# Where matmul operands start in SBUF: moving the tiles of a hybrid decoder block onto multiples of 64 bytes

## The chip, the cores and the metric

The kernel runs on one core of one Trainium2 chip. The metric is the device time of one execution in microseconds, taken as the median of several runs. Two such kernels are compared here: the one called before, and the one that the change makes of it.

## The reference

One decoder block over 1024 tokens and 16 learned meta tokens (1040 in all), model width 1024, in float32. Cut to what matters:

```python
xn = rms_norm(h, norm_mix_g)
q, k, v, f_logit, b_gate, c_gate, u = split(xn @ w_in)       # 1024 -> 3*512 + 8 + 3*512
y_attn = forgetting_attention(q, k, v, log_sigmoid(f_logit + b_f))   # 8 heads of 64, causal
y_conv = b_gate * causal_depthwise_conv(c_gate * u, conv_w)          # 3 taps
h = h + concat(head_rms_norm(y_attn), head_rms_norm(y_conv)) @ w_out
a = square(relu(rms_norm(h, norm_mlp_g) @ w_ff1))                    # 1024 -> 4096
h = h + a @ w_ff2
return rms_norm(h, final_norm_g)[:, 16:]
```

## The kernel before, in words

A product is made of three matmuls. Each float32 operand is split into a high part (rounded to fp32r) and a low part (the rest), by `split` (lines 117 to 119): ScalarE casts the high part, VectorE or GpSimd subtracts. A product then is high times high, high times low and low times high, three matmuls of 128 rows into one PSUM bank, up to 512 columns each. The call is `matmul(out, stationary, moving)`: the stationary operand is a tile of 128 columns that is loaded into TensorE, the moving one is streamed past it. In the rows of the trace the two stand as `out<-moving,stationary`.

The work runs through these stages, which follow each other on TensorE:

- Up to 73 us: the tokens are normed and transposed into `xh` and `xl` (lines 222 to 230), and the values are projected (`value_tile`, line 255).
- 73 to 407 us: the projection of q, k and the three convolution inputs (`project`, line 469), first alone, then as filler between the small matmuls of attention (`scores` lines 531 to 534, `transposed` line 554, `weighted` lines 568 to 570). Here the weights are stationary (`wh`, `wl`) and the tokens move. The tokens of one group are cut into runs of columns by `chunks` (lines 333 to 336): 2 runs of 512 for q and for the convolution's gate, 3 of 348, 348 and 344 for k, 3 of 342 for the convolution's two other inputs, which begin 2 tokens early, at token 14. A run of 3 times 8 matmuls fills one of two PSUM banks named `mm`; after it the run is evacuated by ScalarE and VectorE into a page `pg`.
- 407 to 514 us: the rest of attention, with the convolution's half of the output projection as filler (`out_conv`, line 658).
- 514 to 604 us: the attention half of the output projection (`mixed`, line 863), the norm and the transposes for the MLP (line 877), and the first products of the MLP (`ahead`, line 993).
- 604 to 901 us: the first MLP matrix in Strassen form (`product`, line 993): 1272 matmuls of 512 columns one after the other. The token tiles `xa` to `xd` move, the weights (`wf0`, `ws12`, `ws43`, `wa22`) are stationary.
- 901 to 1205 us: the second MLP matrix in the same form (`second`, line 1298): 1344 matmuls of 512 columns. The weights `w2` move, the activations `a2` are stationary.

What sets the order: within attention the filler is a Python generator; `fill(us)` (lines 692 to 694) draws matmuls from it, and each tells its width over 2400 as its price (line 471), until the slot's quota (tables `QUOTA0` and `QUOTA1`) is used up. From there on TensorE's instructions are kept in the order in which the program names them; on the other engines a scheduler decides where it isn't pinned. The loads of the next group's weights (`wr`, line 329) and the stores of q and k (lines 399 to 415) stand in one queue, SP's.

Where a tile lies: pools take SBUF from the left end upwards, or (with `side="right"`) from the right end downwards, and each tile begins at the next multiple of 32 bytes in its partition. So a tile of an odd number of 32-byte pieces moves all that follow it by 32 bytes. In the program as built, the operands of the 5937 matmuls begin at these remainders by 64 bytes (for a slice of a tile, the slice's own start):

| matmuls | count | moving, stationary |
|---|---|---|
| line 1298: most steps; the second (`ws12`,`wf0`) and the last two | 1272; 72 | 32, 32; 0, 0 |
| line 993, `acc`; `ahead` | 1272; 72 | 32, 0; 32, 32 |
| line 863, `wa`,`y3`; `wa`,`yh` or `yl` | 48; 144 | 32, 0; 0, 0 |
| line 658 | 192 | 0, 0 |
| line 469, 512 columns | 384 | 0, 32 |
| line 469, 342 columns | 576 | 16, 40 or 56; 32 |
| line 469, 348 columns; 344 columns | 192; 96 | 0 or 48, 32; 32, 32 |
| line 255 | 416 | half 0, 0 and half 32, 0 |
| lines 531 and 532 | 224 | 0, 0 (104); 16, 32 or 48, 0 (120) |
| line 554 (transposes) | 320 | 110 at 0, 0; 210 at 0, 32 |

Of the kernel before, what the change touches and what calls it, by code (L numbers as in the profile page):

```python
# [11 lines left out]
F32 = mybir.dt.float32  # L12
F32R = mybir.dt.float32r
# [7 lines left out]
P = 128  # L21
# [15 lines left out]
def r32(ap):  # L37
    return ap.bitcast(F32)
# [3 lines left out]
def hymba_block(  # L42
# [8 lines left out]
    L = T + NM  # L51
    NT = T // P
    KD = D // P
    NH = b_f.shape[1]
# [9 lines left out]
    NK = NT + 1  # L64
    LAST = L - NT * P
    SCALE = HD ** -0.5
    KPAD = 4
# [6 lines left out]
        name=nc.get_next_instruction_name(), act_func_set_id=LN_EXP_SET, ins=[], outs=[]))  # L74

    const = ctx.enter_context(tc.tile_pool(name="const", bufs=1))
    small = ctx.enter_context(tc.tile_pool(name="small", bufs=4))
    scr = ctx.enter_context(tc.tile_pool(name="scr", bufs=1, space=DRAM))

    ident = const.tile([P, P], F32, name="ident")  # L80
    make_identity(nc, ident)
    identb = const.tile([P, P], BF16, name="identb")
# [8 lines left out]
    nc.vector.memset(r32(bones), 0.0)  # L91
    for j in range(2):
        nc.vector.memset(r32(bones[j * HD:(j + 1) * HD, j * HD:(j + 1) * HD]), 1.0)
    epsc = const.tile([P, 1], F32, name="epsc")
    nc.vector.memset(epsc, EPS)
    halfc = const.tile([P, 1], F32, name="halfc")
    nc.vector.memset(halfc, -0.5)
    onec = const.tile([P, 1], F32, name="onec")
    nc.vector.memset(onec, 1.0)
    og = const.tile([P, KD], F32, name="og")  # L100
    cw = const.tile([P, 3, NC], F32, name="cw")
# [4 lines left out]
    def pe(ins):  # L106
        return tc.keep_in_program_order(ins) if ORDERED[0] else ins
# [48 lines left out]
    rp = proj.enter_context(tc.tile_pool(name="rp", bufs=1, reuse_waits="tile"))  # L156
# [10 lines left out]
    early = ExitStack()  # L167
    ep = early.enter_context(tc.tile_pool(name="ep", bufs=1, side="right", reuse_waits="tile"))
    NV = DA + NH
    wvh = ep.tile([P, KD, NV], F32R, name="wvh")  # L170
    wvl = ep.tile([P, KD, NV], F32R, name="wvl")

    tokens = [(xf[t * P:(t + 1) * P], P, NM + t * P) for t in range(NT)] + [(meta_tokens, NM, 0)]
    xts = []
# [113 lines left out]
                load_tokens()  # L288


    lf = rp.tile([P, NK, NH], F32, name="lf")
    nc.vector.scalar_tensor_tensor(out=lf, in0=zt, scalar=-1.0, in1=zt, op0=ALU.mult, op1=ALU.max)
    nc.scalar.activation(lf, lf, AF.Exp, scale=-1.0)
    nc.scalar.activation(lf, lf, AF.Ln, bias=onec)
# [3 lines left out]
    at = ap.enter_context(tc.tile_pool(name="at", bufs=1, side="right", reuse_waits="tile"))  # L298
# [32 lines left out]
        return wh, wl  # L331

    def chunks(lo, n, parts):
        step = -(-n // parts)
        step += step % 2
        return [(lo + i, min(step, n - i)) for i in range(0, n, step)]

    pages = ExitStack()
    pt = pages.enter_context(tc.tile_pool(name="pt", bufs=1, reuse_waits="tile"))
# [11 lines left out]
    def head_norm(src, kt, c, e2=None):  # L351

        st = {}
        s = src[:, c * 512:(c + 1) * 512]

        def squares():
            sq = st["sq"] = at.tile([P, 512], F32, name="n_sq", bufs=1)
            nc.scalar.activation(sq, s, AF.Square)
            st["sh"] = at.tile([P, 512], F32R, name="n_sh", bufs=1)
            st["sl"] = at.tile([P, 512], F32R, name="n_sl", bufs=1)  # L360
            split(st["sh"], st["sl"], sq, nc.gpsimd)

        def scaled():
            ps = bank("mm")
            pe(nc.tensor.matmul(ps, bones, st["sh"], start=True, stop=False))
            pe(nc.tensor.matmul(ps, bones, st["sl"], start=False, stop=e2 is None))
            for t in range(4 if e2 is not None else 0):
                w = e2[:, t].rearrange("p a b -> p (a b)")
                pe(nc.tensor.matmul(ps[:, t * P:(t + 1) * P], w, ident, start=False, stop=t == 3))
            r = st["sq"]  # L370
            nc.scalar.activation(r, ps, AF.Ln, bias=epsc if e2 is None else 0.0, scale=1.0 / HD)
            nc.scalar.activation(r, r, AF.Exp, scale=-0.5)
            y = at.tile([P, 512], F32, name="n_y", bufs=1)
            nc.vector.scalar_tensor_tensor(
                out=y, in0=s, scalar=og[:, kt:kt + 1], in1=r, op0=ALU.mult, op1=ALU.mult)
            if kt < NP - 1:
                nc.sync.dma_start(y_att[c][kt], y)
            elif kt < NP:
                split(y3["h"][:, c * 512:(c + 1) * 512], y3["l"][:, c * 512:(c + 1) * 512], y)
            else:  # L380
                nc.sync.dma_start(y_conv[c][kt - NP], y)

        return [squares, scaled]


    def q_group(p):
        st = {}

        def evac(ps, t0, n):
            if not st:  # L390
                st["h"], st["l"] = page(st), page(st)
            o = slice(t0 - NM, t0 - NM + n)
            hi = st["h"][:, o].bitcast(F32R)
            nc.scalar.mul(hi, ps, SCALE)
            nc.vector.scalar_tensor_tensor(
                out=st["l"][:, o].bitcast(F32R), in0=ps, scalar=SCALE, in1=r32(hi), op0=ALU.mult, op1=ALU.subtract)

        def done():
            nc.sync.dma_start(q_scr[p, 0], st["h"][:, :T])
            nc.sync.dma_start(q_scr[p, 1], st["l"][:, :T])  # L400

        return p * P, chunks(NM, T, 2), evac, done
# [16 lines left out]
    def conv_groups(ct):  # L419
        st = {}  # L420
        p0 = NM - 2
        ch = chunks(p0, T + 2, 3)

        def evac_c(ps, t0, n):
# [71 lines left out]
    def stacks(h):  # L496
        p, j = divmod(h, 2)
        js = slice(j * HD, (j + 1) * HD)
        ka = at.tile([P, L + KPAD], F32R, name="ka", bufs=2)
        kb = at.tile([P, L + KPAD], F32R, name="kb", bufs=2)  # L500
        qa = at.tile([P, T], F32R, name="qa", bufs=2)
        qb = at.tile([P, T], F32R, name="qb", bufs=2)
        for dst, src in ((qa[:HD], q_scr[p, 0, js]), (ka[:HD, :L], k_scr[p, 0, js]),
                         (qa[HD:], q_scr[p, 1, js]), (ka[HD:, :L], k_scr[p, 0, js]),
                         (qb[:HD], q_scr[p, 0, js]), (kb[:HD, :L], k_scr[p, 1, js]),
                         (qb[HD:HD + 4], qrow[h]), (kb[HD:HD + 4, :L], krow[h])):
            nc.sync.dma_start(r32(dst), src)
        nc.gpsimd.memset(r32(ka[:, L:]), 0.0)
        nc.gpsimd.memset(r32(kb[:HD + 4, L:]), 0.0)
        return qa, qb, ka, kb  # L510
# [6 lines left out]
    def scores(i, st, s):  # L517

        qa, qb, ka, kb = st
        n = NM + P * (i + 1)  # L520
        nb = 2 * (i // 2) + 2
        qs = slice(i * P, (i + 1) * P)
        nch = -(-n // 512)
        pad = -n % (2 * nch)
        v = (n + pad) // nch
        w = max(v, 256)
        ps = pp.tile([P, 3, 512], F32, name="S", bufs=BANKS["S"])
        for c in range(nch):
            ks = slice(c * v, c * v + w)
            last = c == nch - 1  # L530
            pe(nc.tensor.matmul(ps[:, c, :w], qa[:, qs], ka[:, ks], start=True, stop=False))  # L531
            pe(nc.tensor.matmul(ps[:, c, :w], qb[:HD + 4, qs], kb[:HD + 4, ks], start=False, stop=not last))  # L532
            if last:
                pe(nc.tensor.matmul(ps[:, c, v - P - pad:v], identb, maskb[:, :P + pad], start=False, stop=True))  # L534
        ps = ps[:, :nch, :v]
        nm = small.tile([P, 1], F32, name="nm")
        nc.vector.tensor_reduce(nm, ps, axis=AX.XY, op=ALU.max, negate=True)  # L537
        pr = at.tile([P, L + KPAD], F32, name="pr", bufs=3)
        if n < nb * P:
            nc.gpsimd.memset(pr[:, n:nb * P], 0.0)  # L540
        nc.scalar.activation(  # L541
            pr[:, :n + pad].rearrange("p (a b) -> p a b", b=v), ps, AF.Exp, bias=nm, accum_out=s)
        return pr
# [31 lines left out]

    def attention_norm(p, c):
        ts = slice(4 * c, 4 * c + 4)
        se = at.tile([P, 4, 2], F32, name="se", bufs=1)
        nc.vector.tensor_scalar(se, sums[p][:, ts], HD * EPS, None, op0=ALU.mult)
        e2 = at.tile([P, 4, 2, HD], F32, name="e2", bufs=1)  # L580
        both = [t.unsqueeze(3).broadcast_to([P, 4, 2, HD]) for t in (se, sums[p][:, ts])]
        nc.gpsimd.tensor_tensor(out=e2, in0=both[0], in1=both[1], op=ALU.mult)
        pending.extend(head_norm(o[p], p, c, e2))
# [116 lines left out]
    ORDERED[0] = True  # L700
    fill(START)
    pr = scores(0, st[0], sums[0][:, 0, 0:1])
    late = None
    for t, (h, i) in enumerate(slots):
# [8 lines left out]
        if t + 1 < len(slots):  # L713
# [5 lines left out]
            pr = scores(i1, st[h1], sums[p1][:, i1, j1:j1 + 1])  # L719
# [230 lines left out]
    for i in range(2, NT):  # L950
        n = i - 2
# [32 lines left out]
    def acc(n=1):  # L984
        return [p2.tile([P, 512], F32, name="acc", tag="acc", bufs=8) for _ in range(n)]
# [120 lines left out]
    n, m = NT - 2, NT - 1  # L1106
# [195 lines left out]
    b = acc(4)  # L1302
# [3 lines left out]
    right = [ctx.enter_context(tc.tile_pool(name=n, bufs=1, side="right", reuse_waits="tile")) for n in ("sr", "r11", "sp")]  # L1306
# [16 lines left out]
    lo, hi = slice(0, HD2), slice(HD2, D)  # L1323
# [56 lines left out]
    for i in range(2, len(steps)):  # L1380
# [14 lines left out]
        if i >= 4 and rowq:  # L1395
            a, tt = rowq.popleft()
# [23 lines left out]
        if q == 0:  # L1420
            b = acc(4)
# [37 lines left out]
```

## Time and profile before

| | |
|---|---|
| median of 3 runs | 1211.78 us (1211.17 to 1214.83) |
| the profiled execution | 1215.61 us, of which the program's span is 1213.5 us |
| mean granted TensorE clock | 0.988 of 2.4 GHz |
| TensorE busy | 1170.1 us, 96% of the span |
| VectorE, ScalarE, GpSimd busy | 729.2, 544.2, 225.8 us |
| matmuls of line 1298, line 469 | 513.6 us, 434.6 us as sums of overlapping durations |

A matmul's duration in these tables runs from its start to the end of its result, and the next one starts before that, so durations overlap. The pace of a run of matmuls is read from the timeline instead: the start of one and the start of another some places later, divided by the number of places.

### The profile page before, as it was taken

How to read it: one execution, taken by the hardware profiler on the slowest of the kernel's cores; microseconds unless marked ns; L12 is line 12 of the kernel's file. 1: busy time of each engine (PE TensorE's matmuls, PEld its weight loads, DVE VectorE, ACT ScalarE, POOL GpSimd, SP SyncE). 2: the span in 40 equal slices, each digit the busy share in tenths (PEclk: the TensorE clock that was granted, in tenths of full speed). 3: DMA queues.
4: the chain of work that ended last, by engine and by line, in shares of the span. 5: the costliest groups of instructions: out<-in, count | busy, mean ns of one | idle time of the engine just before them, and what ended most of it. 6: DMA issues, size and time to landing. Idle time of an engine off the chain costs nothing.

```text
span 1213.5 us, 15649 instructions
## 1 busy us (share of the span) xinstructions
PE 1170.1 (96%) x5969; PEld 987.1 (81%) x5969; DVE 729.2 (60%) x979; ACT 544.2 (45%) x910; POOL 225.8 (19%) x223
## 2 busy tenths in 40 slices
PE   6999999999999899978899999999999999999997
PEld 6988989899988777867788888888888888888886
DVE  7632354435354655549868766666664546985686
ACT  6522334553555554536544343435353433434444
POOL 3011132222221211212533332313100000000000
PEclk9999999999999899989999999999999999999999
DMA  8348242452324564255345444353559756432561
GB/s 259 132 145 234 71 91 57 120 153 61 90 88 141 156 190 130 72 182 182 120 130 191 145 142 165 122 184 102 191 197 363 276 205 228 154 104 70 173 243 70
DMA packets 119978, 185.91 MB, mean 153 GB/s; under 512 B 9536, under 2 KB 61760, under 8 KB 119904
## 3 DMA queue, kind: packets, MB, share of 16 engines
q1 hardware_dynamic: 119904, 184.92, 47.6%
q8 instruction: 47, 0.77, 0.3%
q14 instruction: 27, 0.22, 0.1%
HBM read 126.30 MB, written 58.59 MB: 152 GB/s over the span
## 4 chain that ended last, share of the span: by engine, by line
PE 87%; DVE 5%; DMA 4%; ACT 3%; issue 2%; POOL 0%; SPq 0%; DVEq 0%; ACTq 0%; POOLq 0%
PE acc L1298 25%; PE acc L993 24%; PE mm L469 18%; PE tr L554 3%; PE mm L658 3%; PE wide L863 2%; PE S L255 1%; PE S L531 1%; PE S L532 1%; PE pv L568 1%; PE pv L569 1%; PE mm L255 1%; DMA raw<-y_conv 1%; PE ahead L993 1%; PE pv L570 1%
## 5 line engine op out<-in xcount | busy, mean ns | idle before, releaser
L1298 PE MATMUL acc<-w2h,a2l 128*128 128x512 f32 x440 | 171.2, 389 | 0.0
L1298 PE MATMUL acc<-w2l,a2h 128*128 128x512 f32 x440 | 171.2, 389 | 0.0
L1298 PE MATMUL acc<-w2h,a2h 128*128 128x512 f32 x440 | 171.2, 389 | 0.0
L469 PE MATMUL mm<-xh,wh 128*128 128x342 f32 (+3 forms) x416 | 145.0, 349 | 1.0 <-DVE vm L264 0.8
L469 PE MATMUL mm<-xh,wl 128*128 128x342 f32 (+3 forms) x416 | 144.9, 348 | 0.0
L469 PE MATMUL mm<-xl,wh 128*128 128x342 f32 (+3 forms) x416 | 144.7, 348 | 0.0
L118 ACT CAST a2h<-ar 128x1024 fp32r<-128x1024 f32 x54 | 56.9, 1053 | 147.1 <-PE acc L1298 92.5
L115 DVE TENSOR_TENSOR a2l<-ar,a2h 128x1024 fp32r<-128x1024 f32 x54 | 66.1, 1225 | 86.0 <-ACT a2h L118 85.9
L1298 PEld LDWEIGHTS acc<-w2l,a2h 128*128 128x128 f32 x440 | 82.6, 188 | 17.3
L1298 PEld LDWEIGHTS acc<-w2h,a2h 128*128 128x128 f32 x440 | 82.6, 188 | 17.1
L1298 PEld LDWEIGHTS acc<-w2h,a2l 128*128 128x128 f32 x440 | 82.6, 188 | 17.1
L469 PEld LDWEIGHTS mm<-xh,wh 128*128 128x128 f32 x416 | 78.5, 189 | 7.8 <-DVE vm L264 1.1
L469 PEld LDWEIGHTS mm<-xl,wh 128*128 128x128 f32 x416 | 78.6, 189 | 6.1
L469 PEld LDWEIGHTS mm<-xh,wl 128*128 128x128 f32 x416 | 78.5, 189 | 6.1
L115 DVE TENSOR_TENSOR ptl<-tr,pth 128x512 fp32r<-128x512 f32 (+1 forms) x96 | 56.3, 597 | 37.9 <-ACT pth L118 37.4
L115 POOL TENSOR_TENSOR wl<-wr,wh 128x512 fp32r<-128x512 f32 x40 | 53.5, 1357 | 115.9 <-ACT wh L118 103.9
L786 ACT ACTIVATE ac<-ac 128x1024 f32<-128x1024 f32 (+1 forms) x64 | 66.5, 1040 | 15.1 <-DVE ac L780 14.1
L541 ACT ACTIVATE pr<-S,nm 128x144 f32<-128x144 f32 (+3 forms) x64 | 48.5, 757 | 46.1 <-DVE nm L537 44.6
L118 ACT CAST pth<-tr 128x512 fp32r<-128x512 f32 (+1 forms) x96 | 47.9, 514 | 46.6 <-PE tr L554 34.3
L537 DVE TENSOR_REDUCE nm<-S 128x1 f32<-128x144 f32 (+3 forms) x64 | 49.4, 772 | 24.8 <-PE S L534 24.1
L780 DVE TENSOR_TENSOR ac<-acc,cv 128x512 f32<-128x512 f32 x61 | 41.7, 687 | 32.7 <-PE acc L993 32.5
L118 ACT CAST ws12h<-w1s 128x1024 fp32r<-128x1024 f32 x16 | 16.8, 1050 | 91.7 <-PE acc L993 90.0
(280 smaller groups left out, 2711.5 us busy)
## 6 DMA issues: line engine op xcount, KB each, us to landing
ar<-a_scr SPq DMA_DIRECT2D x54, 512.0 KB
w1r<-in_w_ff_dram SPq DMA_DIRECT2D x16, 1024.0 KB
a_scr<-ac SPq DMA_DIRECT2D x16, 1024.0 KB
a_scr<-sm SPq DMA_DIRECT2D x16, 768.0 KB
w<-in_w_ff_dram SPq DMA_DIRECT2D x24, 512.0 KB
wr<-in_w_in_dram SPq DMA_DIRECT2D x40, 256.0 KB
w2r<-in_w_ff_dram SPq DMA_DIRECT2D x16, 512.0 KB
k_scr<-pg SPq DMA_DIRECT2D x8, 520.0 KB
```

What stands on the lines that cost most here:

```text
L115: pin((eng or nc.vector).tensor_tensor(out=lo, in0=src, in1=r32(hi), op=ALU.subtract))
L118: pin(nc.scalar.copy(hi, src))
L255: pin(nc.tensor.matmul(ps[half], lhs, w_[:, k, f0:f0 + fn], start=k == 0 and a == 0, stop=k == KD - 1 and a == len(terms) - 1))
L469: pe(nc.tensor.matmul(ps, x_[:, k], y_[:, k, ts], start=k == 0 and a == 0, stop=k == KD - 1 and a == 2))
L537: nc.vector.tensor_reduce(nm, ps, axis=AX.XY, op=ALU.max, negate=True)
L541: nc.scalar.activation(pr[:, :n + pad].rearrange("p (a b) -> p a b", b=v), ps, AF.Exp, bias=nm, accum_out=s)
L554: pe(nc.tensor.transpose(ps[:, jj], pr[:, kt * P:(kt + 1) * P], ident))
L658: pe(nc.tensor.matmul(ps, y_[:, k], w_[:, cs], start=k == 0 and a == 0, stop=k == NC - 1 and a == 2))
L780: pin(eng.tensor_tensor(out=out, in0=a, in1=b, op=ALU.add))
L786: pin(nc.scalar.activation(out, src, func, **more))
L993: pe(nc.tensor.matmul(ps, w[w_][:, k], m[m_][:, k], start=k == a == 0, stop=k == HK - 1 and a == 2))
L1298: pe(nc.tensor.matmul(banks[tt], w[w_][:, k, tt * P:(tt + 1) * P], m[m_][:, k], start=first and f == k == a == 0, stop=last and f == len(f ...
```

## The change

Four things change, and all of them move addresses.

1. A pool of one 32-byte tile, `edge`, is opened first at the right end; all tiles of the right side stand 32 bytes lower. The three constants share one tile, so all of the left side behind them stands 64 bytes lower.
2. Tiles that end between two multiples of 64 bytes are made larger, and the added part isn't used: `wvh` and `wvl` by 8 columns of 512+8, `lf` by one block, `ka`, `kb` and `pr` from 1044 to 1056 columns, `se` from 4 to 8 blocks.
3. `chunks` cuts at multiples of 16 tokens: k becomes 352, 352 and 336, the convolution's two inputs 354, 336 and 336; q and the gate keep 512 and 512. The columns of a group stay 1040, 1026 and 1024.
4. Nothing else: the operations, their number and their operands' shapes are the same, but for the widths of item 3 and of the instructions that evacuate these runs.

In the program as built, 5509 of the 5937 matmuls then have both operands at remainder 0: all of lines 863, 993 and 1298, and of line 469 all but the 192 matmuls of 354 columns (56, 0). Of the rest, 140 are at 0, 32 (transposes of line 229, `xm` in line 255, the sums over `bones`), 80 at 32, 0 and 16 at 48, 0 (lines 531 and 532, at cuts that scores make themselves).

```diff
+    edge = ctx.enter_context(tc.tile_pool(name="edge", bufs=1, side="right"))
+    edge.tile([P, 8], F32, name="edge")
...
-    epsc = const.tile([P, 1], F32, name="epsc")
+    consts = const.tile([P, 3], F32, name="consts")
+    epsc, halfc, onec = (consts[:, i:i + 1] for i in range(3))
...
-    wvh = ep.tile([P, KD, NV], F32R, name="wvh")
-    wvl = ep.tile([P, KD, NV], F32R, name="wvl")
+    wvh = ep.tile([P, KD, NV + 8], F32R, name="wvh")[:, :, :NV]
+    wvl = ep.tile([P, KD, NV + 8], F32R, name="wvl")[:, :, :NV]
...
-    lf = rp.tile([P, NK, NH], F32, name="lf")
+    lf = rp.tile([P, NK + 1, NH], F32, name="lf")[:, :NK]
...
     def chunks(lo, n, parts):
-        step = -(-n // parts)
-        step += step % 2
-        return [(lo + i, min(step, n - i)) for i in range(0, n, step)]
+        cuts = [lo] + [-(-(lo + n * i // parts) // 16) * 16 for i in range(1, parts)] + [lo + n]
+        return [(a, b - a) for a, b in zip(cuts, cuts[1:])]
...
-        ka = at.tile([P, L + KPAD], F32R, name="ka", bufs=2)
-        kb = at.tile([P, L + KPAD], F32R, name="kb", bufs=2)
+        ka, kb = (at.tile([P, L + 16], F32R, name=n, bufs=2)[:, :L + KPAD] for n in ("ka", "kb"))
...
-        pr = at.tile([P, L + KPAD], F32, name="pr", bufs=3)
+        pr = at.tile([P, L + 16], F32, name="pr", bufs=3)
...
-        se = at.tile([P, 4, 2], F32, name="se", bufs=1)
+        se = at.tile([P, 8, 2], F32, name="se", bufs=1)[:, :4]
```

The widths enter the filler's prices, so the slots of attention draw a few matmuls more or fewer than before. TensorE's order around the first such place, in a slot of the first head (at 134.6 us in the trace of before; `mm` is the filler's bank, `pr` the probabilities, `tr` their transposes). Before:

```order
L469 MATMUL mm<-xl,wh 128x342
L469 MATMUL mm<-xh,wl 128x342
L559 MATMUL tr<-ident,pr 16x128
L469 MATMUL mm<-xh,wh 128x342
L469 MATMUL mm<-xl,wh 128x342
L469 MATMUL mm<-xh,wl 128x342
L469 MATMUL mm<-xh,wh 128x342
L469 MATMUL mm<-xl,wh 128x342
L469 MATMUL mm<-xh,wl 128x342
L554 MATMUL tr<-ident,pr 128x128 x6
```

Now:

```order
L471 MATMUL mm<-xh,wh 128x336
L471 MATMUL mm<-xl,wh 128x336
L560 MATMUL tr<-ident,pr 16x128
L471 MATMUL mm<-xh,wl 128x336
L471 MATMUL mm<-xh,wh 128x336
L471 MATMUL mm<-xl,wh 128x336
L471 MATMUL mm<-xh,wl 128x336
L471 MATMUL mm<-xh,wh 128x336
L471 MATMUL mm<-xl,wh 128x336
L555 MATMUL tr<-ident,pr 128x128 x6
```

The first piece of filler ends one matmul earlier, so that the same six matmuls behind it begin with another of the three; from there on such shifts of one or two matmuls go on until the projection is done, and on VectorE and ScalarE some evacuations of `mm` change places with a neighbour. From line 863 on, all engines have the order of before.

SP's queue at one of the two places where it changes: the stores of the third pair's q, and the loads of weights `wr` for the group after the next. Before:

```order
L381 DMA y_conv_97<-n_y 128x512
L399 DMA q_scr<-pg 128x1024
L329 DMA wr<-in_w_in_dram 128x4x128
L400 DMA q_scr<-pg 128x1024
L329 DMA wr<-in_w_in_dram 128x4x128
L377 DMA y_att_95<-n_y 128x512
```

Now:

```order
L383 DMA y_conv_99<-n_y 128x512
L332 DMA wr<-in_w_in_dram 128x4x128
L401 DMA q_scr<-pg 128x1024
L332 DMA wr<-in_w_in_dram 128x4x128
L402 DMA q_scr<-pg 128x1024
L379 DMA y_att_97<-n_y 128x512
```

Each of the two loads has moved ahead of a store of q. At the other place, a load of `wr` has moved behind the first load of `qa` for the next head.

## Rows read from the trace of the kernel before

**Rows 1.** The page's shares of the chain that ended last, by engine and line.

```profile
PE 87%; DVE 5%; DMA 4%; ACT 3%; issue 2%; POOL 0%; SPq 0%; DVEq 0%; ACTq 0%; POOLq 0%
PE acc L1298 25%; PE acc L993 24%; PE mm L469 18%; PE tr L554 3%; PE mm L658 3%; PE wide L863 2%; PE S L255 1%; PE S L531 1%; PE S L532 1%; PE pv L568 1%; PE pv L569 1%; PE mm L255 1%; DMA raw<-y_conv 1%; PE ahead L993 1%; PE pv L570 1%
```

**Rows 2.** Windows: stretch, its us, PE, PEld, DVE, ACT, POOL busy (instructions), clock, DMA, GB/s.

```profile
113.00:407.00 294.00, 288.60 (x1765) 259.12 (x1765) 130.87 (x214) 137.43 (x300) 68.88 (x84) 1.00 0.37 102
514.00:604.00 90.00, 76.53 (x334) 60.40 (x334) 68.08 (x82) 46.49 (x82) 27.56 (x20) 0.92 0.51 167
604.00:901.00 297.00, 297.00 (x1274) 239.09 (x1274) 200.41 (x231) 126.83 (x138) 85.28 (x60) 1.00 0.45 152
901.00:1195.00 294.00, 294.00 (x1299) 243.36 (x1298) 199.61 (x202) 121.86 (x139) 2.04 (x2) 1.00 0.58 196
```

**Rows 3.** Views of source lines 993, 1298 and 863: durations min/median/max in ns.

```profile
L993 PE MATMUL acc<-xah,wf0h x104: 395/396/396, 646.1 to 886.2; 128*128 128x512 f32 x104
...
L1298 PE MATMUL acc<-w2h,a2h x440: 387/389/395, 900.9 to 1204.9; 128*128 128x512 f32 x147
...
L863 PE MATMUL wide<-wa,yh x96: 387/389/775, 514.4 to 579.3; 128*128 128x512 f32 x96
L863 PE MATMUL wide<-wa,y3h x32: 392/397/397, 526.8 to 580.0; 128*128 128x512 f32 x32
```

**Rows 4.** Timeline of PE, line 993: start in us, us, what (24 places apart).

```profile
657.26 0.40 PE L993 MATMUL acc<-xbh,ws12h 128*128 128x512 f32 x1
...
662.86 0.40 PE L993 MATMUL acc<-xbh,wa22h 128*128 128x512 f32 x1
```

**Rows 5.** Timeline of PE, line 1298 (12, then 10 and 13 places apart).

```profile
968.93 0.39 PE L1298 MATMUL acc<-w2h,a2h 128*128 128x512 f32 x1
...
971.65 0.39 PE L1298 MATMUL acc<-w2h,a2h 128*128 128x512 f32 x1
...
906.31 0.39 PE L1298 MATMUL acc<-ws12h,wf0h 128*128 128x512 f32 x1
...
908.61 0.39 PE L1298 MATMUL acc<-ws12l,wf0h 128*128 128x512 f32 x1
...
911.55 0.40 PE L1298 MATMUL acc<-ws12h,wf0l 128*128 128x512 f32 x1
```

**Rows 6.** Timeline of PE, line 863 (3, then 9 places apart).

```profile
546.64 0.63 PE L863 MATMUL wide<-wa,y3h 128*128 128x512 f32 x2
...
547.34 0.62 PE L863 MATMUL wide<-wa,yh 128*128 128x512 f32 x2
...
549.38 0.63 PE L863 MATMUL wide<-wa,y3h 128*128 128x512 f32 x2
```

**Rows 7.** Timeline of PE, line 469 (23, then 48, then 25 places apart).

```profile
93.52 0.32 PE L469 MATMUL mm<-xl,wh 128*128 128x344 f32 x1
...
97.13 0.39 PE L469 MATMUL mm<-xh,wh 128*128 128x512 f32 x1
...
108.32 0.32 PE L469 MATMUL mm<-xh,wh 128*128 128x348 f32 x1
...
112.32 0.32 PE L469 MATMUL mm<-xl,wh 128*128 128x348 f32 x1
```

**Rows 8.** Groups by shape, line 469: one of three rows of each shape.

```profile
L469 PE MATMUL mm<-xh,wh 128*128 128x342 f32 x192 | 62.4, 325 | 0.0
...
L469 PE MATMUL mm<-xh,wl 128*128 128x512 f32 x128 | 51.7, 404 | 0.0
```

**Rows 9.** SP's waits from 113 to 407 us (total, times, longest), and SP's timeline.

```profile
SPq L329 <- POOL wl L115: 81.9, 17, 13.7
...
245.46 0.32 SPq L399 DMA_DIRECT2D q_scr<-pg  x1
...
266.60 0.47 SPq L507 DMA_DIRECT2D qa<-q_scr  x1
```

**Rows 10.** The page's group of VectorE's evacuations of transposes.

```profile
L115 DVE TENSOR_TENSOR ptl<-tr,pth 128x512 fp32r<-128x512 f32 (+1 forms) x96 | 56.3, 597 | 37.9 <-ACT pth L118 37.4
```

More of the change, by code (lines that the diff above doesn't have):

```diff
@@ L93, in hymba_block @@
         nc.vector.memset(r32(bones[j * HD:(j + 1) * HD, j * HD:(j + 1) * HD]), 1.0)
-    epsc = const.tile([P, 1], F32, name="epsc")
+    consts = const.tile([P, 3], F32, name="consts")
+    epsc, halfc, onec = (consts[:, i:i + 1] for i in range(3))
     nc.vector.memset(epsc, EPS)
-    halfc = const.tile([P, 1], F32, name="halfc")
     nc.vector.memset(halfc, -0.5)
-    onec = const.tile([P, 1], F32, name="onec")
     nc.vector.memset(onec, 1.0)
```

## The prediction

> **What bounds the kernel now.** I read the chain that ended last first [rows 1]: 87% of it is TensorE, and three source lines make 67% of the span: 1298, 993 and 469. Then the windows [rows 2], to see whether TensorE waits inside these stages. It doesn't: from 604 to 901 us it is busy 297.00 of 297 us, from 901 to 1195 us 294.00 of 294, from 113 to 407 us 288.60 of 294, all at a granted clock of 1.00, the upper level of 2.4 GHz. VectorE, the next busiest, has 200.41 of the 297 us. So in these stages time goes only if the matmuls themselves follow each other faster, and whatever they gain there is gained by the end.
>
> Next I looked at how fast they follow each other, since the counts don't fit: 294 us hold 1299 matmuls of 512 columns, 297 us only 1274 of the same shape [rows 2]. The timeline gives the pace. Line 993: 24 places in 5.60 us, 233.3 ns each [rows 4]. Line 1298: 12 places in 2.72 us, 226.7 ns each [rows 5]. The durations say the same, 396 against 389 ns [rows 3]. In line 993 the moving operand begins at remainder 32 and the stationary one at 0; in line 1298 both begin at 32. That could be the stage and not the address, so the row that decides is one where both kinds stand side by side: line 863 has `yh` and `yl` at 0, 0 and the `y3` ones at 32, 0, in the same bank, one behind the other. Three places at 32, 0 take 0.70 us, 233 ns each; the nine that follow at 0, 0 take 2.04 us, 226.7 ns each [rows 6]. Their median durations are 397 and 389 ns [rows 3]. And line 469, at 0, 32, with ScalarE and VectorE otherwise occupied, takes 48 places in 11.19 us, 233.1 ns [rows 7]. So I read: where the two operands' starts differ by 32 bytes a matmul of 512 columns costs 6.6 ns more than where they agree, and it is no matter which of the two is at 32.
>
> One more thing in rows 5. The 24 matmuls of the second step of line 1298 are at 0, 0 in the middle of a run at 32, 32. Their first ten places take 2.30 us, 230.0 ns each, and only the next thirteen, 2.94 us, 226 ns each. After a break in the pattern the fast pace takes some ten matmuls to come. This is the price between the two that I use below for short runs.
>
> **The change part by part.**
>
> *Line 993.* All 1272 go from 32, 0 to 0, 0: 6.6 ns each, 8.4 us, on the path, since nothing else is waited for there [rows 2]. The other engines have room: the stage would be 288.6 us with VectorE busy 200. The lower bound is the slow start kept for ever, 230.0 ns, thus 3.3 ns each, 4.2 us; I take the upper end, as the run has no break and line 1298 holds 226.7 with as busy a VectorE (199.61 of 294).
>
> *Line 469, 512 columns.* 384 matmuls (three rows of 128 [rows 8]) go from 0, 32 to 0, 0. In attention they run in pieces of 10 to 20 between other matmuls, so part of each is slow start: between 233.1 − 230.0 = 3.1 and 6.4 ns each, 1.2 to 2.5 us; I take the middle, 4.7 ns, 1.8 us.
>
> *Line 469, the narrower runs.* 576 of 342 columns [rows 8] and 192 of 348 begin apart, 96 of 344 agree. Pace: 344 columns 3.61 us in 23 places, 157.0 ns; 348 columns 4.00 us in 25 places, 160.0 ns [rows 7]. Between two agreeing widths a column costs (226.7 − 157.0) / (512 − 344) = 0.415 ns, so four columns explain 1.7 of the 3.0 ns, and starts that differ cost 1.3 ns at this width, not 6.6. The number of columns of a group stays, so the new widths cost nothing by themselves. Of the 864, 96 agreed before and 192 still differ (354 columns, at 56), so 576 × 1.3 ns = 0.7 us. Bounds: nothing, and 576 × 6.6 ns = 3.8 us. I take 0.7, by the rows nearest in shape.
>
> *Line 863.* 48 × 6.6 ns = 0.3 us, in a stage where TensorE is busy 76.53 of 90 us and waits for other engines [rows 2]; I count 0.2, from nothing to 0.3.
>
> *Lines 255, 531, 532, 554.* 208, 120 and 210 matmuls that differ, of 128 to 456 columns. No row prices them apart; at 1.3 ns they would give 0.7 us, and I take nothing, since they stand in short pieces and beside waits.
>
> *Line 1298.* 1272 go from 32, 32 to 0, 0. Both are seen at 226 to 227 ns [rows 5], so nothing.
>
> *The order.* Filler matmuls move by one or two places and some evacuations change places with a neighbour. On SP a load of `wr` moves ahead of a store of q. That load waits for GpSimd's last subtraction on its buffer, at worst 13.7 us [rows 9], and the store behind it with it. But the store went out at 245.46 us and q is loaded back at 266.60 us [rows 9], 21 us later, so the wait fits in. I take nothing for all of it.
>
> Sum: 8.4 + 1.8 + 0.7 + 0.2 = 11.1 us. The profiled execution took 1215.6 us, so its like would take 1204.5; the median of the runs lies 3.8 us lower, so I forecast **1200.7 us**. The best ends together (8.4 + 2.5 + 3.8 + 0.3 + 0.7 = 15.7) give 1196.1, the poor ends (4.2 + 1.2) give 1206.4.
>
> **The rivals.**
>
> *A, slow start stays.* Line 993 has GpSimd at work (85.28 us busy) and line 1298 has not (2.04 us) [rows 2]; if that keeps breaking the pattern, 0, 0 runs at 230 ns: 1211.8 − 5.4 = 1206.4 us. For it: rows 5's first ten places. Against it: those ten ended by themselves. Chance 0.10.
>
> *B, the start makes no difference.* Line 993 is slower for some other reason of its stage, and the change gives nothing: 1211.8 us. Against it stands line 863, where both paces alternate within one bank [rows 6]. The Trainium skill's page "SBUF — State Buffer", section Specifications (TRN2), speaks for B: SBUF is read in lines of 16 bytes, and crossing to a new line is what costs. Every start in lines 863, 993 and 1298 is a multiple of 32, so by that rule all of these matmuls cross the same number of lines and would have one pace; rows 4 to 6 don't agree. Chance 0.05.
>
> *C, the new order costs.* In attention instructions change places with a neighbour 6 times on VectorE and 7 times on ScalarE, as I count in the program as built. If TensorE waited each time for the length of one such neighbour (0.6 us [rows 10]), 7.8 us would be given back: 1208.5 us. Against it: these engines are busy 131 and 137 of 294 us there [rows 2], and two banks take turns. Chance 0.07.
>
> *D, slower.* Agreement at 32 is the fast pair, and 0, 0 was fast in rows 5 and 6 only on the heels of others; in one long run it goes at 233.3 ns. Then line 993 stays as it is and the 1272 matmuls of line 1298 lose 6.6 ns each: 1211.8 + 8.4 = 1220.2 us. It decides at 230 ns: above that pace, line 1298 loses more than line 993 gains. Against it: thirteen places at 226 ns [rows 5]. Chance 0.03.
>
> *E.* Starts are not where the change puts them: the program as built shows 5509 of 5937 at 0, 0, so 0.01, at 1211.8 us.
>
> **How the numbers follow.** The forecast has the remaining 0.74. A measurement of this kernel can tell 0.3% (3.6 us) from no change. The forecast and A are faster by more; of C half; B, E and the other half of C are within 0.3%; D is slower: 0.87, 0.10, 0.03. The range runs from the best ends, 1196, to just beyond A, 1207, and leaves out B, C, D and E, 0.16.
>
> **What would show it.** Right: line 993's durations at 389 ns and 24 places in 5.44 us; the stretch that took 604 to 901 us shorter by 8 us; line 469's 512-column runs below 233 ns; line 1298 as it was. A would show 230 ns in line 993 and GpSimd at work where it falls from the fast pace. B would show 396 ns still. C would show waits of line 469 or 531 for VectorE or ScalarE that aren't there now. D would show line 1298 at 396 ns. The reading is wrong if line 993 gains while line 1298 loses, or if line 469's narrow runs gain like the wide ones.

## The result and the profile after

The changed kernel takes 1203.78 us (median of 4 runs, 1201.03 to 1204.99) where the kernel before takes 1212.66 us (4 runs, 1211.17 to 1214.83): a ratio of 0.9922, 95% interval 0.9898 to 0.9946, 8.9 us less. Timed again later, beside e12 below, it took 1205.09 against 1213.23 us: 0.9938, interval 0.9915 to 0.9960. The forecast was 1200.7 us, so the sign and the range held and the sum was some 2 us too large. The ratios below leave out two executions at a lower granted clock, one of e4 (1400.82 us at 0.774) and one of e8 (1923.07 us at 0.558). Its profiled execution took 1203.17 us, with a span of 1201.2 us at a granted clock of 0.990.

The page after: the shares of the chain that ended last, which answer to [rows 1].

```profile
PE 88%; DVE 5%; DMA 2%; ACT 2%; issue 1%; POOL 1%; SPq 0%; DVEq 0%; ACTq 0%; POOLq 0%
PE acc L1299 25%; PE acc L994 24%; PE mm L471 18%; PE mm L659 3%; PE tr L555 3%; PE wide L864 2%; PE S L258 1%; PE pv L569 1%; PE pv L570 1%; PE S L532 1%; PE S L533 1%; PE mm L258 1%; PE ahead L994 1%; DMA wr<-in_w_in_dram 1%; PE pv L571 1%
```

The chain has the same three lines on top. The lines have moved by one or two: 993 is now 994, 1298 is 1299, 469 is 471, 863 is 864, 658 is 659.

Windows of the changed kernel over the stages of [rows 2], in the same columns.

```profile
113.00:407.00 294.00, 288.32 (x1766) 259.34 (x1765) 130.35 (x214) 137.57 (x300) 70.46 (x84) 1.00 0.36 102
510.00:600.00 90.00, 76.29 (x335) 60.26 (x334) 66.95 (x81) 46.50 (x82) 27.65 (x20) 0.92 0.52 167
600.00:888.00 288.00, 288.00 (x1272) 238.45 (x1271) 202.36 (x231) 126.89 (x138) 85.74 (x60) 1.00 0.47 156
888.50:1182.00 293.50, 293.50 (x1297) 243.02 (x1296) 199.33 (x200) 121.91 (x139) 2.04 (x2) 1.00 0.58 196
```

One row has changed. The first MLP matrix needs 288 us for the matmuls that took 297; the first row, attention with the projection, holds 1766 matmuls in its 294 us where it held 1765. The durations, by source line, answer to [rows 3] and [rows 8]:

```profile
L994 PE MATMUL acc<-xah,wf0h x104: 389/389/389, 640.8 to 874.1; 128*128 128x512 f32 x104
...
L1299 PE MATMUL acc<-w2h,a2h x440: 389/389/393, 888.4 to 1192.3; 128*128 128x512 f32 x147
...
L864 PE MATMUL wide<-wa,yh x96: 387/389/776, 510.3 to 575.2; 128*128 128x512 f32 x96
L864 PE MATMUL wide<-wa,y3h x32: 389/389/397, 522.9 to 575.9; 128*128 128x512 f32 x32
...
L471 PE MATMUL mm<-xh,wl x416: 310/323/497, 73.5 to 399.4; 128*128 128x336 f32 x52, 128*128 128x512 f32 x43, 128*128 128x354 f32 x24, 128*128 128x352 f32 x20
...
L659 PE MATMUL mm<-wc,yh x128: 387/397/794, 405.7 to 508.6; 128*128 128x512 f32 x128
```

Line 994 is at 389 ns, and so are the `y3` matmuls of line 864. Line 471 ends at 399.4 us, as line 469 did. Line 659, whose operands begin at 0, 0 in both kernels, has 397 ns in both. The timeline of PE answers to [rows 4] and [rows 7]: 24 places of line 994, then 48 places of line 471.

```profile
653.99 0.39 PE L994 MATMUL acc<-xbl,ws12h 128*128 128x512 f32 x1
...
659.43 0.39 PE L994 MATMUL acc<-xbl,wa22h 128*128 128x512 f32 x1
...
97.21 0.39 PE L471 MATMUL mm<-xh,wh 128*128 128x512 f32 x1
...
108.33 0.32 PE L471 MATMUL mm<-xh,wh 128*128 128x352 f32 x1
```

Line 994: 5.44 us in 24 places, 226.7 ns, where it was 233.3. Line 471: 11.12 us in 48 places, 231.7 ns, where it was 233.1; over all neighbouring pairs of 512 columns in that line that have no wait between them, the mean of the start-to-start times went from 232.7 to 232.2 ns only. So the gain is that of line 994, and the projection, which was to give 2.5 us, gave nearly none.

The profiled spans differ by 12.3 us, more than the medians. In the timeline the stretch from the first to the last matmul of line 994's `acc` shortens from 296.56 to 288.13 us, 8.4 us; 4.1 us are in the stage before (line 658: 107.2 us from first to last; line 659: 103.1). That stage varies from run to run: the changed kernel's own second profile (e11) has 105.5 us, and e4, where its addresses are those of before, 104.3. No run ties that part to the change.

### The profile page after: what moved, and what is told of

Its sections match the earlier page's. It is cut to its first block, busy times and chain, and to the rows that moved or that the text cites. A ratio compares the mean times of both kernels' runs of the same rounds, so it can differ in the third digit from the quotient of the medians.

```text
span 1201.2 us, 15653 instructions
## 1 busy us (share of the span) xinstructions
PE 1158.9 (96%) x5969; PEld 985.2 (82%) x5969; DVE 729.7 (61%) x979; ACT 545.0 (45%) x910; POOL 228.1 (19%) x223
## 4 chain that ended last, share of the span: by engine, by line
PE 88%; DVE 5%; DMA 2%; ACT 2%; issue 1%; POOL 1%; SPq 0%; DVEq 0%; ACTq 0%; POOLq 0%
PE acc L1299 25%; PE acc L994 24%; PE mm L471 18%; PE mm L659 3%; PE tr L555 3%; PE wide L864 2%; PE S L258 1%; PE pv L569 1%; PE pv L570 1%; PE S L532 1%; PE S L533 1%; PE mm L258 1%; PE ahead L994 1%; DMA wr<-in_w_in_dram 1%; PE pv L571 1%
## 5 line engine op out<-in xcount | busy, mean ns | idle before, releaser
L471 PE MATMUL mm<-xh,wh 128*128 128x336 f32 (+3 forms) x416 | 145.1, 349 | 1.3 <-DVE vm L267 0.8
L471 PE MATMUL mm<-xl,wh 128*128 128x336 f32 (+3 forms) x416 | 145.1, 349 | 0.0
L471 PE MATMUL mm<-xh,wl 128*128 128x336 f32 (+3 forms) x416 | 144.5, 347 | 0.0
L787 ACT ACTIVATE ac<-ac 128x1024 f32<-128x1024 f32 (+1 forms) x64 | 66.5, 1041 | 13.3 <-DVE ac L781 12.3
```

Source lines behind the costliest of these rows:

```text
L471: pe(nc.tensor.matmul(ps, x_[:, k], y_[:, k, ts], start=k == 0 and a == 0, stop=k == KD - 1 and a == 2))
L787: pin(nc.scalar.activation(out, src, func, **more))
```

## The experiments

Two questions: is it the distance between the two starts that counts in line 994, and why did the projection not follow?

### How near must the starts be: e1 to e5

In the program as built, line 994's operands both begin at remainder 192 by 256 bytes, and 1296 of line 1299's too. An unused tile ahead of the token tiles moves `xa` to `xd` and what is allocated behind them on the right side; of line 994's 1272 `acc` matmuls it moves the moving operand alone. e1, e2, e3 and e5 are the changed kernel with 32, 64, 128 and 256 bytes of it, e4 is the kernel before with 32 bytes. (The lines move to 996 and, in e4, to 995.)

```diff
+    pad = xs.enter_context(tc.tile_pool(name="pad", bufs=1, side="right"))
+    pad.tile([P, 8], F32, name="pad")
     bx = xs.enter_context(tc.tile_pool(name="bx", bufs=1, side="right", reuse_waits="tile"))
```

e1: 

> The changed kernel with an unused tile of 32 bytes ahead of the MLP's token tiles, so that in line 993's product the tokens begin at remainder 32 and the weights at 0, as before; all else stays as changed. Theory (starts that differ cost a 512-column matmul 6.6 ns): this stage's 1272 matmuls fall back to 233.3 ns each, 396 ns in duration, and the kernel gets 8.4 us slower than the changed one, about the time of before (ratio to before 1.000, within 0.003). Rival (the gain came from the new cuts and the new order of attention, or from evacuations and transfers that land better): the stage keeps 226.7 ns and the ratio to before stays at 0.992.

e2: 

> The same with a tile of 64 bytes: tokens and weights of that product both begin on multiples of 64 bytes, but 64 bytes apart by 256. Theory 64 (agreement by 64 bytes is all that counts): 226.7 ns a matmul, 389 ns in duration. Theory 256 (agreement by 256 bytes counts, which all fast matmuls of both kernels have and line 469 has not): about 233 ns, 395 ns in duration.

e3: 

> The same with a tile of 128 bytes: the starts are 128 bytes apart by 256. Theory 64: 226.7 ns. Theory 256: about 233 ns. If 64 bytes apart is slow and 128 apart is fast, agreement by 128 bytes is what counts.

e4: 

> The kernel before with nothing changed but the same unused 32 bytes ahead of the MLP's token tiles: both operands of line 993's product now begin on multiples of 64 bytes (64 bytes apart by 256), attention and its cuts are those of before. Theory 64: the stage drops to 226.7 ns, 8.4 us, ratio to before 0.993: this one shift is the whole of the change's gain. Theory 256: the pace stays near 233 ns and the ratio is 1.000. Rival (cuts and order of attention): ratio 1.000 as well, with the pace at 233 ns.

e5: 

> The changed kernel with 256 unused bytes ahead of the token buffers. In its first product of the feed-forward the moving and the stationary operand now begin at the same remainder of 256 bytes, at remainders of 512 that differ by 256. If starts have to agree by 256 bytes: 226.7 ns a place, the stage 288.1 us from its first to its last matmul, the whole about 1204 us. If they have to agree by 512 bytes: 231 to 233.3 ns a place, the stage 294 to 296.6 us, the whole 1209 to 1213 us. If any shift away from the changed kernel's own layout costs, for some reason other than the starts: 233.3 ns too.

Measured, with the pace as the mean start-to-start time of neighbours in the line that have no wait between them, and the stage as the time from its first to its last matmul:

| | starts by 256: moving, stationary | pace, ns | stage, us | time, us |
|---|---|---|---|---|
| before | 224, 0 | 233.3 | 296.6 | 1212.66 (4 runs) |
| changed | 192, 192 | 226.7 | 288.1 | 1203.78 (4 runs) |
| e1 | 160, 192 | 233.3 | 296.6 | 1212.43, ratio to before 0.9994 (0.9979 to 1.0008) |
| e2 | 128, 192 | 233.3 | 296.6 | 1210.99 (1 run) |
| e3 | 64, 192 | 232.4 | 295.3 | 1208.38 (1 run) |
| e4 | 192, 0 | 233.3 | 296.6 | 1213.47, ratio to before 1.0004 (0.9987 to 1.0021) |
| e5 | 192, 192 | 226.7 | 288.2 | 1201.78 (1 run) |

The windows bear it out by count. e1, 295 us inside the stage:

```profile
602.00:897.00 295.00, 295.00 (x1266) 237.46 (x1266) 200.44 (x230) 125.33 (x137) 84.88 (x60) 1.00 0.46 151
```

The window of e2, as long:

```profile
600.00:895.00 295.00, 295.00 (x1266) 237.70 (x1265) 200.58 (x230) 125.74 (x137) 84.67 (x59) 1.00 0.46 151
```

The window of e3:

```profile
598.00:893.00 295.00, 295.00 (x1271) 239.21 (x1270) 201.63 (x231) 125.88 (x138) 85.17 (x60) 1.00 0.46 151
```

The window of e4:

```profile
602.00:897.00 295.00, 295.00 (x1266) 237.69 (x1265) 199.39 (x230) 125.28 (x137) 85.24 (x60) 1.00 0.45 151
```

And the window of e5, 288 us long:

```profile
598.50:886.50 288.00, 288.00 (x1272) 238.48 (x1271) 202.09 (x231) 126.91 (x138) 85.57 (x60) 1.00 0.47 155
```

1266 matmuls in 295 us are 233.0 ns each, 1272 in 288 us 226.4 (a window also counts the matmuls that it cuts at its edges, so this comes out a little below the pace in the table). e1 gives back the whole gain by an empty tile of 32 bytes. Other tiles behind the empty one move with the tokens, but e5 moves the same tiles, by 256 bytes, and keeps the gain: so it is where the start lies that counts, and not that tiles were moved. e2 gives the gain back too, with every start of the line on a multiple of 64, and e4 wins nothing though its starts are all on multiples of 64. So it isn't enough that both agree by 32 or 64 bytes, nor by 128 (e3). In e5 they agree by 256 bytes but are 256 apart by 512, and the pace is the fast one: 256 bytes is what counts. The Trainium skill's page "SBUF — State Buffer", section Specifications (TRN2), has lines of 16 bytes, which would give these five kernels one pace; the rows have 226.7 to 233.3 ns.

### Why the projection gained nothing: e6 to e10

In line 471 the moving operand is a row of `xh` or `xl` (one row for each k, the 8 blocks of 128 that a product is added up from), and these rows are 4160 bytes long, 16 times 256 and 64 more. So from one k to the next, every three matmuls, the moving start goes on by 64 bytes, while the stationary one (rows of 512) stands still: by 256 bytes they agree in a quarter of the matmuls. e7 and e8 make both go on together, e9 makes both stand still and agree, e10 makes both stand still apart. All need room in SBUF, which is taken from a weight block that is loaded ahead of `out_conv`; e6 is the control that takes only that.

```diff
-        raws = after["raws"] = [tw.tile([P, D], F32, name=f"ahead{k}") for k in range(NC)]
+        raws = after["raws"] = [tw.tile([P, D if k < NC - 1 else 512], F32, name=f"ahead{k}") for k in range(NC)]
...
-            nc.sync.dma_start(raws[k], wo[(NP + k) * P:(NP + k + 1) * P])
+            nc.sync.dma_start(raws[k], wo[(NP + k) * P:(NP + k + 1) * P, :raws[k].shape[-1]])
...
+        rest = op.tile([P, 512], F32, name="raw", bufs=2)
+        nc.sync.dma_start(rest, wo[(NP + NC - 1) * P:(NP + NC) * P, 512:])
...
```

e6: 

> The changed kernel, in which half of the last weight block of the output projection is loaded when that stage begins and not ahead of it, which frees 2 KB of each partition. A control for the next two runs, whose padding needs the room: no start of a matmul in the input projection changes against the changed kernel. Both theories: the input projection as in the changed kernel (336 columns 154.3 ns, 512 columns 231 to 233 ns), first product of the feed-forward 226.7 ns, the whole 1202 to 1206 us. If the later load is waited for, up to 2 us more in the output projection.

Measured: 1206.97 us, ratio to before 0.9944 (0.9929 to 0.9959). The projection takes 326.4 us from first to last matmul, as in the changed kernel; the matmuls of `out_conv` take 105.7.

e7 adds to e6:

```diff
-        wh = rp.tile([P, KD, P], F32R, name="wh", bufs=2)
-        wl = rp.tile([P, KD, P], F32R, name="wl", bufs=2)
+        wh = rp.tile([P, KD, P + 16], F32R, name="wh", bufs=2)[:, :, :P]
+        wl = rp.tile([P, KD, P + 16], F32R, name="wl", bufs=2)[:, :, :P]
```

e7: 

> The control with the input projection's weight blocks in rows of 576 bytes, not 512, so that the stationary start moves by 64 bytes from one k to the next, as the moving start does already. The starts of all 384 matmuls of 512 columns agree by 256 bytes, and differ by 256 of 512; those of the narrower ones all differ, by the same amount throughout a run. If starts have to agree by 256 bytes: 226.7 ns at 512 columns, 384 x 5 ns = 1.9 us less than the control; narrower runs unchanged or, since a quarter of them agreed before, up to 0.3 us more. If by 512 bytes: 512 columns stay at 231 to 233.3 ns, the whole as the control. If the pace of the input projection has nothing to do with starts: as the control too, but then the run before this one has to show 233 as well.

e8 adds the cuts:

```diff
-        cuts = [lo] + [-(-(lo + n * i // parts) // 16) * 16 for i in range(1, parts)] + [lo + n]
+        cuts = [lo] + [(lo + n * i // parts + 16) // 64 * 64 + 16 for i in range(1, parts)] + [lo + n]
```

e8: 

> As the run before, and the column runs of the input projection cut at tokens of which the remainder by 64 is 16, so that nearly all runs but the first of a group agree by 256 bytes: 384 matmuls of 512 columns (agree by 256, differ by 512), 288 of 384 and 288 of 320 columns (agree by 512 too); 96 of 336 and 192 of 322 columns still differ. If starts have to agree by 256 bytes: 226.7 ns at 512 columns, and at 384 and 320 columns the line through 226.7 at 512 with 0.415 ns a column, 173.6 and 147.0 ns, against some 1.3 ns more for starts that differ; together 384 x 5 + 576 x 1.3 ns = 2.7 us below the control, about 1201 us. If by 512 bytes: only the 0.7 us of the narrower runs, about 1203 us. If starts don't matter in this stage: as the control, 1203.8 us.

Measured: e7 1209.66 us (1 run), its projection 326.1 us; e8 1205.56 us, ratio 0.9930 (0.9912 to 0.9947), its projection 325.6 us. For the projection that is what the theory of 512 bytes expected, which e5 had excluded; the theory of 256 bytes missed. (e7 as a whole is 2.7 us above the control, which no theory expected: in its profile the matmuls of `out_conv` take 109.9 us, in the stage that varies from run to run, and no run ties that to the padding.) In e7 all 384 matmuls of 512 columns agree by 256 bytes, and the undisturbed run of 48 goes so (timeline of PE):

```profile
97.11 0.39 PE L471 MATMUL mm<-xh,wh 128*128 128x512 f32 x1
...
108.21 0.32 PE L471 MATMUL mm<-xh,wh 128*128 128x352 f32 x1
```

11.10 us, 231.2 ns, near the 231.7 of the changed kernel. From the thirteenth place on the trace repeats 224, 231, 236, 237, 232, 230 ns: a period of six matmuls, or two k, with a mean of 231.7. Agreement alone doesn't do it, then, where the starts go on every three matmuls.

So e9: e6 with a quarter instead of half of the block ahead, the cuts of e8, and rows of 4352 bytes, 17 times 256:

```diff
-    xh = rp.tile([P, KD, L], F32R, name="xh")
-    xl = rp.tile([P, KD, L], F32R, name="xl")
+    xh = rp.tile([P, KD, L + 48], F32R, name="xh")[:, :, :L]
+    xl = rp.tile([P, KD, L + 48], F32R, name="xl")[:, :, :L]
```

e9: 

> The control e6 with the rows of the input projection's activations padded from 4160 to 4352 bytes, a multiple of 256, and the same cuts as e8; the room is taken from the last weight block of the output projection, of which now a quarter and not half is loaded ahead. In e8 the starts agreed, but both moved by 64 bytes from one k to the next, and the pace stayed at 231 to 232 ns. Here both stand still at 0 of 256 through a whole run, for 384 matmuls of 512, 288 of 384 and 288 of 320 columns. If starts have to agree and to stay the same from one matmul to the next: 226.7 ns at 512 columns, together 384 x 5 + 576 x 1.3 ns = 2.7 us off the 326.4 us that the projection takes from its first to its last matmul in the control. If the pace of this stage comes from its surroundings (evacuations, GpSimd's subtractions, DMA into the same memory): 231 to 232 ns, and 326 us as before. The whole: 1204 us by the first, 1207 us by the second, up to 2 us more by either if the later load is waited for.

Its timeline, the first, the seventh and the last of the same run of 48 matmuls:

```profile
96.56 0.39 PE L471 MATMUL mm<-xh,wh 128*128 128x512 f32 x1
...
97.94 0.39 PE L471 MATMUL mm<-xh,wh 128*128 128x512 f32 x1
...
107.24 0.39 PE L471 MATMUL mm<-xh,wl 128*128 128x512 f32 x1
```

The first six places take 229 to 236 ns each; the next 41 take 9.30 us, each of them 226 or 227 ns, to the end of the run. That is line 994's pace, in the stage that was to be too disturbed for it. One row of line 471 shows where the stage ends:

```profile
L471 PE MATMUL mm<-xh,wl x416: 303/334/501, 73.3 to 397.8; 128*128 128x512 f32 x43, 128*128 128x320 f32 x32, 128*128 128x384 f32 x29, 128*128 128x322 f32 x24
```

The last of them starts at 397.8 and not at 399.4 us; from first to last matmul it takes 325.1 us, 1.3 less than in the control, where 2.7 was expected. The whole: 1204.06 us, ratio 0.9926 (0.9909 to 0.9943).

e10 keeps the long rows and the cuts and moves the weight blocks by 64 bytes (the block ahead loses as much):

```diff
-    lf = rp.tile([P, NK + 1, NH], F32, name="lf")[:, :NK]
+    lf = rp.tile([P, NK + 3, NH], F32, name="lf")[:, :NK]
```

e10: 

> e9 with 64 unused bytes ahead of the input projection's weight blocks (taken from the block that is loaded ahead): rows of 4352 bytes as in e9, so the starts stand still through a run, but the moving and the stationary one differ by 192 of 256 bytes. If agreement counts as well as standing still: 233.3 ns at 512 columns in the undisturbed run of 48 at 97 us, as in the feed-forward's first product with the same distance, and the projection back at 326 us or more. If the longer row alone made e9 fast: 226.7 ns as in e9.

Its timeline, over 47 places of the same run:

```profile
96.95 0.39 PE L471 MATMUL mm<-xh,wh 128*128 128x512 f32 x1
...
107.92 0.39 PE L471 MATMUL mm<-xh,wl 128*128 128x512 f32 x1
```

10.97 us, 233.4 ns, and the projection takes 326.4 us again (1205.04 us in all, 1 run). e10 has the long rows and the cuts of e9, so it is the agreement that made e9 fast. The four cases stand side by side in one line and one stage, by the undisturbed run of 48:

| starts by 256 bytes | agree | don't agree |
|---|---|---|
| stand still | e9: 226.7 ns after six places | e10: 233.4 ns |
| go on by 64 every three matmuls | e7: 231.2 ns (both go on) | changed kernel: 231.7 ns (one goes on, a quarter agree); before: 233.1 ns (one goes on, none agrees) |

### Is e9 better than the change: e11 and e12

e11 is the changed kernel and e12 is e9, both as they are, timed on one chip.

e11: 

> The changed kernel as it is, beside e12 on the same chip. Both theories: 1203 to 1205 us, as measured before.

e12: 

> e9 as it is, beside e11 on the same chip: is it better than the changed kernel? Its projection took 1.3 us less than that of the changed kernel in one profile each, its later load cost up to 2.6 us in the control. If both hold in full, it is 1 us slower than e11; if the load costs nothing, 1.3 us faster; either is near what 5 rounds can tell.

Measured: e11 1205.09 us (0.9938, 0.9915 to 0.9960), e12 1201.67 us (0.9913, 0.9893 to 0.9932). The intervals overlap, though five of e12's six runs lie below all six of e11's. With the earlier runs, the changed kernel has a median of 1204.4 over 10 runs and e9 with e12 of 1202.6 over 12. The gain of 1.3 us in the projection is there in both profiles of the padded kernel (325.1 and 325.1 us against 326.4 and 326.4); that the whole is faster by it is likely and not shown, and the 3.4 us between the two medians are more than the projection accounts for.

## Why the prediction was right, and where it was wrong

*Line 993, 8.4 us:* right to the tenth. The pace went from 233.3 to 226.7 ns, the stage from 296.6 to 288.1 us, with the other engines as busy as before. Rival A (the slow start stays) and rival D (0, 0 is slow in long runs) fall with it: line 994 holds the fast pace with GpSimd busy 85.74 of 288 us, and line 1299 holds its 389 ns. Rival B falls with e1: the same stage, the same order, 32 bytes further, and the gain is gone.

*The rule behind it* was wrong: "where the two operands' starts differ by 32 bytes a matmul of 512 columns costs 6.6 ns more than where they agree". Only remainders by 64 were compared, and in lines 863, 993 and 1298 these tell the same story as remainders by 256: line 993 was at 224, 0, line 1298 at 224, 224, its second step at 0, 0. The change puts line 994 at 192, 192, and that, not the multiple of 64, is why it won. On other multiples of 64 it would have won nothing (e2, e4) or 1.3 us (e3), and the prediction asked only for a multiple of 64. So the size was read rightly from the rows, but that the new addresses agree by 256 was luck. Nor is it shown that "it is no matter which of the two is at 32": the example the other way round was line 469, whose starts don't stand still.

*Line 469, 512 columns, 1.8 us:* the step that failed. The pace fell by 0.5 ns over all pairs, 384 × 0.5 = 0.2 us, and not by 4.7; from its first to its last matmul the projection takes 326.6 us before and 326.4 after. Its starts agree by 64 in the changed kernel, but by 256 only in a quarter of the cases, and they don't stand still. The trace of before could have warned: line 658 is at 0, 0 there, even by 256, in pieces of at most seven matmuls but for one of 17, and its median is 397 ns as it is after.

```profile
L658 PE MATMUL mm<-wc,yh x128: 387/397/796, 405.7 to 512.7; 128*128 128x512 f32 x128
```

What e9 recovers fits the slow start of the prediction: 3.3 ns a matmul over all pairs (232.2 to 228.9), 384 × 3.3 = 1.3 us, two thirds of the 5.0 ns between the changed kernel's undisturbed run and e9's steady pace; of the 384 matmuls 74 stand in pieces of five or fewer and 228 in pieces of 9 to 20, and in the undisturbed run six places go by before the pace is steady.

*Line 469, narrower runs, 0.7 us:* nothing to be seen. The 1.3 ns read off at 348 columns were taken for the distance of the starts, against 344 columns as a width that agrees; but by 256 only a quarter of those 344-column matmuls agree, and their starts go on. At 384 and 320 columns, e9 (agree) and e10 (apart) differ by 0.7 and 0.3 ns (175.2 against 174.5, 146.6 against 146.3).

*Line 863, 0.2 us:* its `y3` matmuls did become fast (397 to 389 ns), and the stage took 65.8 us from first to last matmul in both profiles: it was spent waiting.

*The order, nothing:* right. The projection ends at 399.4 us in both, and TensorE's longest waits in the stretch of [rows 2]'s first line, those for ScalarE's probabilities, add up to 2.5 us in both. Rival C falls. E does too: the starts are where the change puts them.

So 8.4 of the forecast 11.1 us came, and 2.7 didn't; the measured difference of the medians, 8.9 us in the first timing and 8.1 in the second, has 8.4 between them.

## What to carry to other kernels

Where long runs of 512-column float32 matmuls set the time, compare the remainders of the moving and the stationary start by 256 bytes, not by 32 or 64, and look at the rows' strides as well: here a stride of 64 bytes more than a multiple of 256 made the start go on with every k and took the fast pace away even where both agreed. Expect the gain (2.8% here) only in runs well over ten matmuls long, and check it by the pace in the timeline, line by line: one shifted tile is enough to lose it. A law read off two remainders should be tried on a third line of the same trace before it is given a price elsewhere.

## What the runs showed of the hardware that was not expected

- The pace of a 512-column matmul of this kernel, each with a weight load of its own, depends on the remainder by 256 bytes of the distance between the two operands' starts. It is steady at 226.7 ns where they agree, at 232.4 where they are 128 bytes apart (e3), and at 233.3 to 233.4 where the moving start lies 32 or 64 bytes below the stationary one (before, e1, e2, e4, e10). The other way round was not run with starts that stand still.
- The pace has a memory. After a change of the starts, or after other matmuls, it goes through 224 to 236 ns and settles within nine places (six in e9's undisturbed run, nine at the start of line 994); where the starts change every three matmuls it never settles, but repeats a pattern of six (e7) or twelve matmuls (the changed kernel), both with a mean of 231.7 ns.
- Even the fast pace lies above what the Trainium skill's page "TensorE: Matmul & The Clock Gate" gives for matmuls without a pause (section "Wait — 56ns, not 53.3ns?": the columns over 2.4 GHz and some 2.5 ns, 215.7 ns at 512). No run here shows that pace. What in the chip makes the start of one operand matter to the other was not tried.
